# Products of ones on TensorE during the first loads, column sums of squares taken part by part, and late vectors loaded in the second step

## The chip, the cores and the metric

One core of a Trainium2 chip. The metric is the device time of one execution in microseconds. Below, PE is TensorE, DVE is VectorE, ACT is ScalarE, POOL is GpSimd and SP is SyncE, which issues most of the transfers.

## What is computed

One layer of a diffusion backbone over 512 latent tokens and 256 context tokens of width 1024, all in float32. The part that matters here is its beginning:

```
mod   = silu(c) @ w_ada + b_ada          # 6 x 1024: shift, scale, gate, twice
mod_c = silu(c_ctx) @ w_ada + b_ada
h     = rms_norm(x, norm1_g)   * (1 + scale1)   + shift1
hc    = rms_norm(ctx, norm1_g) * (1 + scale1_c) + shift1_c
q_c, kv_c, k_rope, ... = split(h @ w_in)         # 384, 256, 32, ... columns
q  = rms_norm(q_c,  q_norm_g)  @ w_uq
kv = rms_norm(kv_c, kv_norm_g) @ w_ukv           # the same for the context's kv
```

Attention over 8 heads, a gated linear attention branch, the merge of both, and a feed-forward with a 3x3 depthwise convolution (`conv_w`, `conv_b`) follow; they take most of the time and are not touched.

## The kernel before, in words

Every large product is made of three: each float32 operand is split into a high part (cast, on ScalarE) and a low part (subtraction, on VectorE or GpSimd), and `mm3` (line 144) multiplies high by high, high by low and low by high. `mm` (line 149) is one plain float32 product.

Lines 539 to 667 are the first stage, and its order is written out by hand: with an engine's name in `pinned`, the wrapper around every instruction (line 88) keeps it behind the engine's previous one. All five queues are pinned there; SP until line 667, POOL until 1026, VectorE and ScalarE until 1036, TensorE to the end. What is not pinned is placed by a scheduler. All operations come from that wrapper, so that the profile gives them line 88 (or 87), and tiles tell them apart.

The stage goes over eight slices j of 128 features. For each, `load_ada(j)` and `load_w(j)` issue two parts of `w_ada` (512 KB each) and the q and kv columns of `w_in` (320 KB) on SP, up to three steps ahead. `modulation(j)` (line 489) makes 8 float32 products of `silu(c)` with each part, in four column strips; VectorE copies the result; `factors(j)` (line 500) turns it with two small products into shift and scale per feature. `columns` (line 509) transposes the normalised tokens, `modulated` (line 517) applies shift and scale on ScalarE and splits on VectorE. `kv_latents` and `q_latents` (lines 528 and 533) accumulate the 256 kv columns in `accK` (two banks) and the 384 q columns in `accQ` (two banks, also called `two[1]`) and `accR`. `split_latents(j)` (line 389) splits the weights: casts on ScalarE, subtractions on POOL. Step 0 is done in two halves of 256 tokens (lines 572 to 592): modulation, transposes of two token rows, factors, 15 products of 256 columns; then the token rows 2 and 3 are normalised (lines 579 to 583), and the same again.

The small vectors come as rows into one tile `X0`: `c`, `c_ctx`, `norm1_g` and `b_ada` (ROWS[0:4]) issued on ScalarE, `q_norm_g`, `kv_norm_g`, `gla_norm_g`, `gla_b_decay`, `norm2_g` and `conv_b` (ROWS[4:], together 22 KB) and the two parts of `conv_w` (99 KB) on POOL, all at the start (lines 540 and 551). TensorE transposes the first 16 rows (line 555), the first 72 (line 566), and in step j = 3 the late ones (line 639). Neither kind of transpose nor the products wait for anything but their own operands and the instruction ahead of them.

After the loop (line 930), the squares of the kv latents are added over the two blocks and summed over the features with products by a column of ones (`totals`, line 674: one column per 128 tokens); `spread` (line 669) turns the reciprocal roots into rows. The same follows for q (three blocks, added on VectorE) and for the context's kv (two blocks in one bank), whose sums go into the last columns of `two[1]`, the bank that holds the second block of the q latents. `misc` (line 695) multiplies the rope and decay columns between them.

```
sk, sq = [EK() for _ in range(2)], []                                    # line 930
for k in range(2):
    A.activation(sk[k][:, 0:512], kb_[k], AF.Square)
tt(V, sk[0][:, 0:512], sk[0][:, 0:512], sk[1][:, 0:512], ALU.add)
...
totals(two[1][:, 512:], sq[0], 4)                                        # line 964
totals(two[1][:, 516:], sc, 2)
misc(0, 3, 8)
```

`smask` is the second half of the tile `WD`; the linear attention fills it with ones and zeros (line 1052) and reads it after the attention heads.

Of the kernel before, what the change touches and what calls it, by code (L numbers as in the profile page):

```python
# [13 lines left out]
ALU = mybir.AluOpType  # L14
# [56 lines left out]
def block_kernel(ctx: ExitStack, tc: tile.TileContext, p, out):  # L71
# [58 lines left out]
    def f(ap):  # L130
        return ap.bitcast(F32)
# [17 lines left out]
    def mm(o, a, b, first=True, last=True):  # L149
        PE.matmul(o, lhsT=a, rhs=b, start=first, stop=last)  # L150
# [184 lines left out]
    with tc.tile_pool(name="e1", bufs=1) as e1:  # L335
# [11 lines left out]
        G.memset(f(WD), 0.0)  # L347
# [141 lines left out]
        def modulation(j):  # L489
            for i in range(2):  # L490
                for rnd in range(2):
                    for g in range(4):
                        kt = 2 * g + rnd
                        mm(mp[32 * g:32 * g + 32, 128 * i:128 * i + 128], cstat[:, kt, :], ada[j][i][:, kt, :], rnd == 0,
                           rnd == 1)
            rows = EP()[:, 0:256]
            V.tensor_copy(rows, mp[:, 0:256])
            return rows
# [39 lines left out]

        pinned |= {"PE", "V", "A", "G", "SY"}
        for i_, (name, k) in enumerate(ROWS):  # L540
            load_rows((A if i_ < 4 else G), name, k)
# [9 lines left out]
        for (dst, a, b) in ((pw[:, 0, :], 0, 128), (pw[0:70, 1, :], 128, 198)):  # L551
            G.dma_start(out=dst, in_=p["conv_w"][0].rearrange("a b (c d) -> (a b c) d", d=128)[a:b])

        ps_ = single[1]
        PE.transpose(ps_[:, 0:16], pk[0:16, :], ident[0:16, 0:16])
        cc = pcol[:, 0:16]
# [9 lines left out]
        PE.transpose(single[2][:, 0:NROW1], pk[0:NROW1, :], ident[0:NROW1, 0:NROW1])  # L566
        V.tensor_copy(pcol[:, 16:NROW1], single[2][:, 16:NROW1])
# [6 lines left out]
        factors(0, rows)  # L574
        split_latents(0)
# [22 lines left out]
        def extra_loads(j):  # L598
            if j == 1:
                load_ada(4)  # L600
# [29 lines left out]
        for j in range(1, 8):  # L630
# [8 lines left out]
            if j == 3:  # L639
                ps_ = single[2 - tps[0] % 2]  # L640
                n2 = NROWS - NROW1
                PE.transpose(ps_[:, 0:n2], pk2[0:n2, :], ident[0:n2, 0:n2])
                PE.transpose(ps_[:, 128:256], pw[:, 0, :], ident)
                PE.transpose(ps_[:, 256:326], pw[0:70, 1, :], ident[0:70, 0:70])
                V.tensor_copy(pcol[:, NROW1:NROWS], ps_[:, 0:n2])
                V.tensor_copy(cwT, ps_[:, 128:326])
# [27 lines left out]
        def totals(ss, sq, n):  # L674

            for t in range(n):
                mm(ss[:, t:t + 1], sq[:, t * 128:(t + 1) * 128], ones[:, 0:1])
# [255 lines left out]
        tt(V, sk[0][:, 0:512], sk[0][:, 0:512], sk[1][:, 0:512], ALU.add)  # L933
        q_latents(7, 0, 512)
        mwh, mwl = split_misc(mraw_[0])
        totals(sums, sk[0], 4)
# [15 lines left out]
        for k in range(2):  # L952
            V.scalar_tensor_tensor(out=kn[k][:, 0:512], in0=kb_[k], scalar=col("kv_norm_g", k), in1=rb[:, 0:512],
                                   op0=ALU.mult, op1=ALU.mult)
            A.copy(kvLh[:, k, :], kn[k][:, 0:512])
# [3 lines left out]
        sc = EK()  # L959
        A.activation(sc[:, 0:512], single[1], AF.Square)  # L960
        tt(V, sc[:, 0:256], sc[:, 0:256], sc[:, 256:512], ALU.add)
        q_latent(1)
        q_latent(2)
        totals(two[1][:, 512:], sq[0], 4)
        totals(two[1][:, 516:], sc, 2)
        misc(0, 3, 8)
        scaled(vq[:, 0:4], two[1][:, 512:516], 384)
        scaled(vq[:, 4:6], two[1][:, 516:518], 256)
# [82 lines left out]
    with tc.tile_pool(name="egl", bufs=1) as eg:  # L1051
        G.memset(smask, 1.0)
        G.memset(grp(smask, 4)[:, :, 0:1], 0.0)
        one_c = ones[:, 0:1].broadcast_to([128, 256])
# [512 lines left out]
```

## Time and profile before

| | |
|---|---|
| median of 3 runs | 915.4 us (912.56 to 915.64) |
| the profiled execution's own time | 913.15 us |
| its span, first to last instruction | 911.4 us |
| TensorE busy in the span | 886.5 us (97%) |
| VectorE, ScalarE, GpSimd busy | 580.1, 396.3, 372.6 us |
| mean granted clock of TensorE | 0.995 of full speed |

The profile shows one execution. Times in its rows count from the first instruction. A matmul's end is modelled and contains its way through the array, so the time of a stretch of products is read from start to start. The weight loads that go with the products have rows of their own and are left out here.

### The profile page before, as it was taken

How to read it: one execution, taken by the hardware profiler on the slowest of the kernel's cores; microseconds unless marked ns; L12 is line 12 of the kernel's file. 1: busy time of each engine (PE TensorE's matmuls, PEld its weight loads, DVE VectorE, ACT ScalarE, POOL GpSimd, SP SyncE). 2: the span in 40 equal slices, each digit the busy share in tenths (PEclk: the TensorE clock that was granted, in tenths of full speed). 3: DMA queues.
4: the chain of work that ended last, by engine and by line, in shares of the span. 5: the costliest groups of instructions: out<-in, count | busy, mean ns of one | idle time of the engine just before them, and what ended most of it. 6: DMA issues, size and time to landing. Idle time of an engine off the chain costs nothing.

```text
span 911.4 us, 12634 instructions
## 1 busy us (share of the span) xinstructions
PE 886.5 (97%) x4864; PEld 750.7 (82%) x4864; DVE 580.1 (64%) x971; ACT 396.3 (43%) x655; POOL 372.6 (41%) x223
## 2 busy tenths in 40 slices
PE   5999999999999999999999999999999999999996
PEld 4878899888888888888887889888888888888885
DVE  4567778874967777765674684988787776300006
ACT  4355667764344554534545333443333333322105
POOL 3422255460525252423554423343535444466403
PEclk9999999999999999999999999999999999999998
DMA  9940000216313233324972512434343432244102
GB/s 313 328 131 1 1 4 12 91 47 185 97 42 110 76 104 82 97 78 136 316 252 82 151 47 91 122 111 139 93 138 93 139 115 94 70 161 143 43 1 92
DMA packets 131436, 100.89 MB, mean 111 GB/s; under 512 B 6826, under 2 KB 121874, under 8 KB 131376
## 3 DMA queue, kind: packets, MB, share of 16 engines
q1 hardware_dynamic: 130256, 97.56, 34.9%
q0 software_dynamic: 864, 2.22, 0.7%
q8 instruction: 38, 0.62, 0.3%
q10 hardware_dynamic: 256, 0.30, 0.1%
q14 instruction: 22, 0.18, 0.1%
HBM read 97.78 MB, written 2.10 MB: 110 GB/s over the span
## 4 chain that ended last, share of the span: by engine, by line
PE 90%; DVE 4%; ACT 2%; issue 1%; POOL 1%; DMA 1%; SPq 0%; DVEq 0%; ACTq 0%; POOLq 0%
PE pb L88 47%; PE p L88 23%; PE pb L87 14%; PE p L87 6%; DVE s L88 1%; DMA raw<-in_w_ada_dram 1%; DVE kT L88 1%; ACT s L88 1%; ACT P L88 0%; DVE P L88 0%; DVE mx L88 0%; ACT kT L88 0%; POOL P L88 0%; POOL s L88 0%; POOL wlo L88 0%
## 5 line engine op out<-in xcount | busy, mean ns | idle before, releaser
L88 POOL TENSOR_TENSOR wlo<-raw,whi 128x1024 fp32r<-128x1024 f32 (+1 forms) x106 | 241.6, 2286 | 355.3 <-ACT whi L88 341.2
L88 PE MATMUL pb<-s,whi 128*128 128x512 f32 (+1 forms) x906 | 272.4, 383 | 0.0
L88 PEld LDWEIGHTS pb<-s,whi 128*128 128x128 f32 x906 | 167.6, 188 | 32.1
L88 ACT CAST whi<-raw 128x1024 fp32r<-128x1024 f32 (+1 forms) x106 | 103.4, 977 | 179.6 <-issue 77.6
L88 PE MATMUL pb<-s,wlo 128*128 128x512 f32 (+1 forms) x453 | 172.9, 382 | 0.0
L88 DVE SCALAR_TENSOR_TENSOR ac<-pb,cwT,ac 128x441 f32<-128x441 f32 (+2 forms) x160 | 111.0, 694 | 19.2 <-ACT ac L88 15.4
L87 PE MATMUL pb<-s,whi 128*128 128x512 f32 x320 | 101.7, 396 | 0.0
L88 PEld LDWEIGHTS pb<-s,wlo 128*128 128x128 f32 x453 | 85.3, 188 | 16.6
L88 PE MATMUL p<-s,s 128*128 128x512 f32 (+1 forms) x392 | 83.4, 369 | 1.7 <-DVE s L88 1.5
L88 PEld LDWEIGHTS p<-s,s 128*128 128x128 f32 x392 | 66.4, 191 | 14.9 <-DVE s L88 2.2
L87 PEld LDWEIGHTS pb<-s,whi 128*128 128x128 f32 x320 | 58.9, 188 | 12.4 <-issue 0.7
L88 PE MATMUL p<-whi,s 128*128 128x512 f32 x208 | 69.0, 393 | 0.1
L88 DVE TENSOR_TENSOR p<-p,gt 128x512 f32<-128x512 f32 x4 | 2.8, 699 | 98.5 <-PE p L88 98.4
L87 PE MATMUL pb<-s,wlo 128*128 128x512 f32 x160 | 62.8, 392 | 0.0
L88 PE MATMUL pb<-whi,s 128*128 128x512 f32 x176 | 57.6, 390 | 0.0
L88 PEld LDWEIGHTS p<-whi,s 128*128 128x128 f32 x208 | 39.1, 188 | 8.4 <-ACT s L88 0.4
L88 PE MATMUL pb<-s,s 128*32 128x128 f32 (+2 forms) x322 | 43.6, 335 | 0.9 <-DVE rv L88 0.9
L88 DVE TENSOR_TENSOR pl<-pb,ph 128x512 fp32r<-128x512 f32 x48 | 33.0, 687 | 14.8 <-ACT ph L88 14.5
L88 PE MATMUL p<-kT,s 128*128 128x512 f32 (+1 forms) x192 | 41.1, 350 | 0.9 <-ACT P L88 0.9
L88 PE MATMUL p<-wlo,s 128*128 128x512 f32 x104 | 40.5, 390 | 0.0
L88 ACT ACTIVATE ac<-ac 128x512 f32<-128x512 f32 x22 | 13.9, 632 | 59.6 <-DVE ac L88 59.6
L88 PEld LDWEIGHTS pb<-s,s 128*128 128x128 f32 (+1 forms) x322 | 34.1, 166 | 6.4 <-DVE rv L88 1.1
(250 smaller groups left out, 1558.4 us busy)
## 6 DMA issues: line engine op xcount, KB each, us to landing
raw<-in_w_up_dram SPq DMA_DIRECT2D x44, 512.0 KB, 3.7
raw<-in_w_in_dram SPq DMA_DIRECT2D x28, 512.0 KB, 3.7
raw<-in_w_down_dram SPq DMA_DIRECT2D x22, 512.0 KB, 3.6
s<-in_w_ada_dram SPq DMA_DIRECT2D x20, 512.0 KB, 5.9
raw<-in_w_ada_dram SPq DMA_DIRECT2D x18, 512.0 KB, 5.1
xn<-in_w_ada_dram SPq DMA_DIRECT2D x10, 512.0 KB, 5.1
kT<-in_w_in_dram SPq DMA_DIRECT2D x8, 320.0 KB, 6.9
s<-in_x_dram SPq DMA_DIRECT2D x4, 512.0 KB, 5.3
```

What stands on the lines that cost most here:

```text
L87: return fn(*args, **kw)
L88: ins = fn(*args, **kw)
```

## The change

Four kinds of edits. Thirteen float32 products of ones with ones (`fill`, into `accK`, which is begun anew before it is used) are placed between the first instructions of TensorE; the ones are `smask`, now filled by VectorE at the start, while POOL clears only the other half of `WD`. The rows ROWS[4:] and `conv_w` are issued by POOL in step j = 1, behind the subtractions of step 2's weights, and their transposes stand in step j = 5. The sums of squares of kv and of the context take the two blocks as two accumulating products instead of an addition on VectorE and one product; the context's squares are taken earlier on ScalarE; the sums of q and context go into `sums`. And the two instructions that fill `smask` for the linear attention are pinned.

```diff
--- before.py
+++ after.py
@@ -344,7 +344,8 @@
         pk, pk2, pw = X0[:, 0:128], X0[:, 128:256], grp(X0[:, 256:512], 2)
         kcos, ksin = tl(e1, [128, 512], F32, "pl", 2), tl(e1, [128, 512], F32, "pl", 2)
         V.memset(cstat, 0.0)
-        G.memset(f(WD), 0.0)
+        V.memset(smask, 1.0)
+        G.memset(f(wst), 0.0)
 
         def load_rows(eng, name, k):
             src = p[name]
@@ -488,6 +489,8 @@
 
         def modulation(j):
             for i in range(2):
+                if j == 0 and i == 1:
+                    fill(accK, 1, 128)
                 for rnd in range(2):
                     for g in range(4):
                         kt = 2 * g + rnd
@@ -536,9 +539,14 @@
                 ws = slice(k * 128, (k + 1) * 128)
                 mm3(qb_[k][:, a:b], wj[j][0][:, ws], wj[j][1][:, ws], h_, l_, j == 0 and a == 0, j == 7)
 
+        def fill(ps, n, width=256):
+
+            for _ in range(n):
+                mm(ps[:, 0:width], smask[:, 0:128], smask[:, 0:width])
+
         pinned |= {"PE", "V", "A", "G", "SY"}
-        for i_, (name, k) in enumerate(ROWS):
-            load_rows((A if i_ < 4 else G), name, k)
+        for name, k in ROWS[0:4]:
+            load_rows(A, name, k)
         SY.dma_start(out=cst[:, 0:130], in_=p["consts"][:, 0:130])
         load_x(0)
         load_x(1)
@@ -548,11 +556,12 @@
         load_x(3)
         load_ada(1)
         load_w(1)
-        for (dst, a, b) in ((pw[:, 0, :], 0, 128), (pw[0:70, 1, :], 128, 198)):
-            G.dma_start(out=dst, in_=p["conv_w"][0].rearrange("a b (c d) -> (a b c) d", d=128)[a:b])
-
+
+        fill(accK, 3)
+        fill(accK, 1, 128)
         ps_ = single[1]
         PE.transpose(ps_[:, 0:16], pk[0:16, :], ident[0:16, 0:16])
+        fill(accK, 2)
         cc = pcol[:, 0:16]
         V.tensor_copy(cc, ps_[:, 0:16])
         se, sc_ = sm(16, "se", 1), sm(16, "sc_", 1)
@@ -564,6 +573,7 @@
         tt(V, cstat[:, :, 1], cc[:, 8:16], sc_[:, 8:16], ALU.mult)
         ss = squared(0)
         PE.transpose(single[2][:, 0:NROW1], pk[0:NROW1, :], ident[0:NROW1, 0:NROW1])
+        fill(accK, 1)
         V.tensor_copy(pcol[:, 16:NROW1], single[2][:, 16:NROW1])
         for dst, j in ((b1sc, 8), (b2sc, 32)):
             V.tensor_scalar(out=dst, in0=pcol[:, ROW0["b_ada"] + j:ROW0["b_ada"] + j + 8], scalar1=1.0, scalar2=None,
@@ -572,6 +582,7 @@
         rows = modulation(0)
         tp = columns(0, 0, 0, 2)
         factors(0, rows)
+        fill(accK, 5, 128)
         split_latents(0)
         modulated(0, 0, 0, 2, tp)
         kv_latents(0, 0, 256)
@@ -597,6 +608,10 @@
 
         def extra_loads(j):
             if j == 1:
+                for name, k in ROWS[4:]:
+                    load_rows(G, name, k)
+                for (dst, a, b) in ((pw[:, 0, :], 0, 128), (pw[0:70, 1, :], 128, 198)):
+                    G.dma_start(out=dst, in_=p["conv_w"][0].rearrange("a b (c d) -> (a b c) d", d=128)[a:b])
                 load_ada(4)
                 load_w(4)
                 load_x(4)
@@ -636,7 +651,7 @@
                 V.tensor_scalar(out=xs[j], in0=xs[j], scalar1=rc[:, j - 4:j - 3], scalar2=None, op0=ALU.mult)
             elif j == 7:
                 context(4, 8)
-            if j == 3:
+            if j == 5:
                 ps_ = single[2 - tps[0] % 2]
                 n2 = NROWS - NROW1
                 PE.transpose(ps_[:, 0:n2], pk2[0:n2, :], ident[0:n2, 0:n2])
@@ -674,7 +689,8 @@
         def totals(ss, sq, n):
 
             for t in range(n):
-                mm(ss[:, t:t + 1], sq[:, t * 128:(t + 1) * 128], ones[:, 0:1])
+                for i, s_ in enumerate(sq):
+                    mm(ss[:, t:t + 1], s_[:, t * 128:(t + 1) * 128], ones[:, 0:1], i == 0, i == len(sq) - 1)
 
         def scaled(v, ss, width):
             V.tensor_scalar(out=v, in0=ss, scalar1=-0.5 / width, scalar2=-0.5 * EPS, op0=ALU.mult, op1=ALU.add)
@@ -930,10 +946,9 @@
         sk, sq = [EK() for _ in range(2)], []
         for k in range(2):
             A.activation(sk[k][:, 0:512], kb_[k], AF.Square)
-        tt(V, sk[0][:, 0:512], sk[0][:, 0:512], sk[1][:, 0:512], ALU.add)
         q_latents(7, 0, 512)
         mwh, mwl = split_misc(mraw_[0])
-        totals(sums, sk[0], 4)
+        totals(sums, sk, 4)
         scaled(vk, sums[:, 0:4], 256)
         ctx_latents(0, 4)
         sq.append(EK())
@@ -952,20 +967,20 @@
         for k in range(2):
             V.scalar_tensor_tensor(out=kn[k][:, 0:512], in0=kb_[k], scalar=col("kv_norm_g", k), in1=rb[:, 0:512],
                                    op0=ALU.mult, op1=ALU.mult)
+            if k == 0:
+                sc = EK()
+                A.activation(sc[:, 0:512], single[1], AF.Square)
             A.copy(kvLh[:, k, :], kn[k][:, 0:512])
         for k in range(2):
             sub(V, kvLl[:, k, :], kn[k][:, 0:512], f(kvLh[:, k, :]))
         misc(0, 0, 3)
-        sc = EK()
-        A.activation(sc[:, 0:512], single[1], AF.Square)
-        tt(V, sc[:, 0:256], sc[:, 0:256], sc[:, 256:512], ALU.add)
         q_latent(1)
         q_latent(2)
-        totals(two[1][:, 512:], sq[0], 4)
-        totals(two[1][:, 516:], sc, 2)
+        totals(sums, sq[0:1], 4)
+        totals(sums[:, 4:], [sc, sc[:, 256:]], 2)
         misc(0, 3, 8)
-        scaled(vq[:, 0:4], two[1][:, 512:516], 384)
-        scaled(vq[:, 4:6], two[1][:, 516:518], 256)
+        scaled(vq[:, 0:4], sums[:, 0:4], 384)
+        scaled(vq[:, 4:6], sums[:, 4:6], 256)
         rq = rstd_exp(None, 6, None, vq)
         split_wq(2)
         spread(sums, rq[:, 4:6], 2)
@@ -1049,8 +1064,10 @@
     G.dma_start(out=gt1, in_=p["b_ada"][0:1, 2048:3072].broadcast_to([128, 1024]))
 
     with tc.tile_pool(name="egl", bufs=1) as eg:
+        pinned.add("G")
         G.memset(smask, 1.0)
         G.memset(grp(smask, 4)[:, :, 0:1], 0.0)
+        pinned.discard("G")
         one_c = ones[:, 0:1].broadcast_to([128, 256])
 
         def E2(tag, n, bufs):
```

## Rows read from the trace of the kernel before

**Rows 1.** The page's chain of work that ended last, as shares of the span by engine.

```profile
PE 90%; DVE 4%; ACT 2%; issue 1%; POOL 1%; DMA 1%; SPq 0%; DVEq 0%; ACTq 0%; POOLq 0%
```

**Rows 2.** Timeline of TensorE, first 40 us. Columns: start (us), time to the end of the last of the group (us), engine, line, operation, output<-inputs, stationary rows*columns, shape of the moving part, count, and in brackets the idle time before and what ended it. A group merges equal instructions in a row; an f32 product is two instructions, a transpose one.

```profile
4.96 0.25 PE L88 MATMUL pb<-cst,X 16*128 16x16 f32 x1 [4.96 <-DMA X<-in_c_ctx_dram]
7.87 0.35 PE L88 MATMUL pb<-cst,X 72*128 72x72 f32 x1 [2.65 <-DMA X<-in_b_ada_dram]
9.12 1.08 PE L88 MATMUL pb<-s,s 128*32 128x128 f32 x16 [0.90 <-DVE rv L88]
10.70 1.08 PE L88 MATMUL pb<-raw,s 128*32 128x128 f32 x16 [0.50 <-DMA raw<-in_w_ada_dram]
...
12.33 1.02 PE L88 MATMUL pb<-cst,P 128*128 128x2 f32 x4
14.83 1.90 PE L88 MATMUL p<-s,s 128*128 128x256 f32 x6 [1.49 <-DVE s L88]
...
18.58 1.08 PE L88 MATMUL pb<-s,s 128*32 128x128 f32 x16
...
20.45 1.20 PE L88 MATMUL pb<-cst,s 128*128 128x128 f32 x6
...
22.12 1.32 PE L88 MATMUL p<-s,s 128*128 128x256 f32 x6
...
24.36 0.60 PE L88 MATMUL pb<-cst,s 128*128 128x128 f32 x4
24.89 0.65 PE L88 MATMUL pb<-s,s 128*32 128x128 f32 x16
...
25.90 1.66 PE L88 MATMUL p<-s,s 128*128 128x512 f32 x6
27.40 0.50 PE L88 MATMUL pb<-cst,P 128*128 128x2 f32 x4
...
37.43 1.64 PE L88 MATMUL p<-s,s 128*128 128x512 f32 x6
```

**Rows 3.** Timeline of VectorE (DVE), first 45 us, same columns.

```profile
10.09 1.42 DVE L88 TENSOR_SCALAR s<-s,rr 128x1024 f32<-128x1024 f32 x2
11.85 0.42 DVE L88 COPY P<-pb 128x256 f32<-128x256 f32 x1 [0.35 <-PE pb L88]
13.39 0.22 DVE L88 TENSOR_SCALAR shc<-pb,pcol 128x2 f32<-128x2 f32 x1 [1.11 <-PE pb L88]
...
14.81 0.43 DVE L88 TENSOR_TENSOR s<-P,s 128x256 fp32r<-128x256 f32 x1
...
18.62 0.75 DVE L88 TENSOR_SCALAR s<-s,rr 128x1024 f32<-128x1024 f32 x1
```

**Rows 4.** Timeline of TensorE, 60 to 85 us, same columns.

```profile
65.18 1.05 PE L88 MATMUL pb<-ones,kT 128*128 128x1 f32 x8 [0.90 <-DVE kT L88]
66.10 3.12 PE L88 MATMUL pb<-s,s 128*128 128x256 f32 x24
...
76.49 1.50 PE L88 MATMUL p<-ones,kT 128*128 128x1 f32 x12 [1.26 <-DVE s L88]
77.85 5.28 PE L88 MATMUL pb<-s,s 128*128 128x512 f32 x15
82.96 1.50 PE L88 MATMUL pb<-cst,rr 128*128 128x128 f32 x12
```

**Rows 5.** Windows view of two stretches: from:to (us), length, busy time of PE, PEld, DVE, ACT and POOL with the number of instructions, granted clock of TensorE as a share of full speed, DMA share, GB/s.

```profile
40.00:50.00 10.00, 10.00 (x104) 7.98 (x104) 6.72 (x14) 4.40 (x10) 5.58 (x7) 1.00 1.05 306
...
80.00:81.00 1.00, 1.00 (x4) 0.81 (x3) 0.79 (x2) 0.00 (x0) 0.00 (x0) 0.50 0.00 0
```

**Rows 6.** Timeline of TensorE around the one f32 product of 256 columns with ones in the feed-forward stage (`mod_bcast`).

```profile
607.13 0.39 PE L88 MATMUL pb<-s,wlo 128*128 128x512 f32 x1
607.36 0.59 PE L88 MATMUL pb<-mp,ones 128*128 128x256 f32 x2
...
608.25 0.40 PE L88 MATMUL pb<-s,wlo 128*128 128x512 f32 x1
```

**Rows 7.** Timeline of SyncE's issues (SPq): start, time the issue held the queue, transfer.

```profile
8.91 2.19 SPq L88 DMA_DIRECT2D raw<-in_w_ada_dram  x1
```

**Rows 8.** The view of one tensor, `in_w_ada_dram`, first 60 us: from issue to landing, of 16 transfers.

```profile
DMA to landing us min/median/max: 5.2/6.9/8.1
```

**Rows 9.** Timeline of GpSimd (POOL), first 45 us, columns as in rows 2; a DMA row is the time that the issue takes on GpSimd.

```profile
24.93 1.45 POOL L88 TENSOR_TENSOR wlo<-kT,whi 128x384 fp32r<-128x384 f32 x1
29.59 0.74 POOL L88 TENSOR_TENSOR s<-kT,s 128x256 fp32r<-128x256 f32 x1 [3.20 <-ACT s L88]
...
44.52 0.73 POOL L88 DMA_DIRECT2D qtab<-in_consts_dram  x1
```

**Rows 10.** Timeline of VectorE, 64 to 77 us.

```profile
64.44 0.68 DVE L88 TENSOR_TENSOR kT<-kT,kT 128x512 f32<-128x512 f32 x1
...
75.22 0.42 DVE L88 TENSOR_TENSOR kT<-kT 128x256 f32<-128x256 f32 x1
75.68 0.75 DVE L88 SCALAR_TENSOR_TENSOR s<-p,pcol,s 128x512 fp32r<-128x512 f32 x1
```

**Rows 11.** Timeline of ScalarE (ACT), 71 to 75 us.

```profile
71.64 0.59 ACT L88 COPY P<-pb 128x512 f32<-128x512 f32 x1
...
74.48 0.60 ACT L88 ACTIVATE kT<-pb 128x512 f32<-128x512 f32 x1
```

## The prediction

> **What bounds the kernel now.** I read the chain of waits first. TensorE holds 90% of what ended last [rows 1], so the end moves only where TensorE idles, runs at a lower clock, or gets more or less work. I then looked for those places in its timeline. There are two.
>
> The first is the start [rows 2]. Up to 14.83 us TensorE waits for small loads, weights and VectorE: 4.96, 2.65, 0.90, 0.50 and 1.49 us of idle time ahead of the rows shown. From there the work is dense, but slow. The 15 products of 14.83 to 18.58 us take 3.75 us; the same 15 from 22.12 to 24.36 us take 2.24 us; both include a short wait for the low half, a subtraction of 0.43 us [rows 3]. The 32 modulation products take 1.87 us from 18.58 us and 1.01 us from 24.89 us. 15 x 256 columns in 3.75 us less 0.4 are 1.15 columns per ns, about the lower of the two clock levels, 1.2 GHz; afterwards the rate is about double. (The granted clock shows no value below 1.00 in this stretch, so I go by the durations.) The rise thus comes near 22 us, after some 7 us of dense products.
>
> The second is 64 to 83 us, where the latents' squares are summed [rows 4]. TensorE waits 0.90 us for an addition of squares, later 1.26 us for VectorE, and soon after that the granted clock is 0.50 [rows 5]: 15 products of 512 columns take from 77.85 to 82.96 us, 5.11 us. At the upper level one takes 0.23 us (607.13 to 607.36 us, [rows 6]), 15 take 3.4; the lower level costs 1.7 us.
>
> **The fills, and what they cost.** 13 products of ones are added: six 256 wide, seven 128 wide. The nearest row is the f32 product with ones, 256 columns wide, in the feed-forward: from 607.36 to 608.25 us there lie this product and two of 0.225 us, so it takes 0.44 us at the upper level [rows 6]; I put 0.88 us at the lower, and half of each for 128 columns. All 13 are 8.4 us at the lower level and 4.2 us at the upper, against 10.5 us of idle time. Group by group at the lower level, the ones being ready near 1.7 us (VectorE is idle there, so their memset costs nothing): three and a half end at 4.8 us, before the load of 4.96 us; two from 5.2 us end at 7.0, before 7.87; one from 8.2 us ends at 9.1, at the 9.12 us product; the small one between the halves of the modulation ends at 10.5, before 10.70. The last five lie behind the factors: at the lower level they run from 13.35 to 15.5 us, 0.7 us past the start of the 14.83 us products; at the upper from 12.5 to 13.6 us, and cost nothing. Only products behind them on TensorE wait for a fill.
>
> **What they bring.** I take the clock to be up by 11 to 14 us, since from 8.2 us on fills, transposes and modulation leave almost no gap; the bound on the other side is a rise near 22 us as now. With it up, the first modulation ends near 11.3 us, the copy of its rows follows VectorE's scaling, at 11.5 us instead of 11.85 [rows 3], the factors take 0.5 us as at 27.40 us (1.02 at 12.33, [rows 2]), and their readers on VectorE start at 12.55 instead of 13.39 us. So the products of 14.83 us start at 14.0. What is late next is not TensorE: its 15 and 32 products would be through at 17.3 us, but rows three and four of x are normalised behind the factors' readers on ScalarE and VectorE, to 19.37 us now [rows 3], to 18.5 us then. The transposes of 20.45 us start at 18.55, 1.9 us earlier; they and what follows are 0.3 us shorter, so 24.36 us becomes 22.15. I put **2.2 us**. Bounds: 0.7 us lost (the five fills late, no rise) and 3.5 us won (both stretches at double rate, no chain in the way).
>
> Do the loads allow it? The modulation weights issued at 8.91 us [rows 7] land at most 8.1 us later [rows 8], at 17.0 us, just where they would be used then; later ones are issued up to three steps ahead. A wait of 0.3 us here would lie inside the 18.5 us that VectorE sets.
>
> **The row loads.** Eight issues leave GpSimd's first microseconds (121 KB) and return behind its low-half subtractions of step 2, which end at 26.4 us now, 24.2 then [rows 9]. At 0.73 us each, the longest such row, they end at 30.0 us. The next subtraction, due at 27.4 us then, waits behind them and ends at 30.8 us; its reader, the product of 37.43 us [rows 2], then at 35.2, has 4 us left. The transposes that read the rows move two steps on, to about 46 us, 8 us after the last landing. Early on, 121 KB at the 306 GB/s of [rows 5] are at most 0.4 us less ahead of the first weights; between 0 and 0.4 I take 0, since the chain above goes by x, which is issued ahead of most of them. GpSimd's smaller memset and its pinned later one lie in idle time.
>
> **The sums of squares.** First place: the addition of 0.68 us goes [rows 10], and the column sums double from 8 to 16 instructions of 0.115 us (0.92 us for 8, [rows 4]): from 64.28 they end at 66.1, as now. Nothing is gained; VectorE comes 0.68 us earlier, and TensorE does not wait for it there. Second place: the sums go into a bank that VectorE reads until 76.43 us [rows 10], hence the 1.26 us. The new bank has its last reader at 71.64 to 72.23 us [rows 11]. The context squares move ahead on ScalarE, from 74.48 us to about 73.3; the high halves behind them slip 0.6 us, and VectorE, rid of an addition of 0.42 us, reaches its q latents as now. So the sums start at 75.2 and their 16 instructions (12 now) end at 77.0 instead of 77.85: **0.9 us**. The scale factors are ready near 78.5 us, and the products in between hold TensorE until 80.5, so no new wait. Bounds: 1.3 us (the whole gap) and nothing.
>
> **The clock there.** After 64.28 us there are 1.8 us without dense products, and the clock stayed up; after 75.2 there are 2.6, and it fell. With 1.8 us in the second place too, I take it to stay: **1.7 us**, with 0 as the other end.
>
> **Sum.** 2.2 + 0.9 + 1.7 = 4.8 us off the profiled execution's 913.15: 908.3. The median of the runs shown lies 2.25 us above that execution, and the runs spread over 3.1 us; a clock that rises or falls at another moment could do that, and the fills should take part of it away. I put 910.0, between 908.3 and the median less 4.8, 910.6.
>
> The Trainium skill, "TensorE: Matmul & The Clock Gate", Part 1, says that the lower rate is the default and activity releases it, with which the start agrees. A remark there puts the ramp at under 1% of a typical span and warns against fitting it to one count; by it the 2.2 us could be anything from nothing to 3.5 us, which the range holds.
>
> **Rivals.** *The clock falls again in the second place.* Sixteen one-column instructions in a row remain there, and one stretch that stayed up is thin evidence. Then the 1.7 us stay: 911.7. *The fills don't bring the rise forward.* Until 8 us they leave gaps of 0.9 us, and the nearly dense 14.83 to 18.23 us brought no rise by itself. Then the start gains nothing: 912.2; with both, 913.9. *Slower: GpSimd's issues take far longer in step 2*, with the DMA queues full, than at the start; SyncE's issue at 8.91 us took 2.19 us [rows 7]. From 1.3 us per issue on, the subtraction of step 3 ends after 35.2 us and TensorE waits; at 2.2 us each it ends at 42.5, 7 us late, and the time is 917; at 2.6 us, 920.5. Against it: the issue of 44.52 us took 0.73 us [rows 9], with the DMA share at 1.05 and VectorE busy for 6.7 of 10 us [rows 5]. The Trainium skill, "DMA: Bandwidth & Descriptors", section SWDGE vs HWDGE vs iDMA, says that GpSimd writes its descriptors into memory out of which VectorE can lock it; by that page this rival would be likelier. That row does not show it.
>
> **How the numbers follow.** Forecast 0.50; second fall 0.20; no earlier rise 0.15; both 0.07; GpSimd's issues 0.05; something else 0.03. Range 906.5 to 914.7: below, 908.3 with a start 1.3 us better and 0.4 us of loads; above, both rivals and 0.8 us. About 0.5% (4.6 us) is what a measurement of this kernel can tell from no change; faster by that is under 910.8. Of the forecast 0.36 lie there, of the second fall 0.06, of the late rise 0.03: 0.45 in all. Slower by it is over 920: 0.05 with what is unforeseen. Same: 0.50.
>
> **What would show it.** Right: the first 15 products in little over 2 us; the transposes of 20.45 us near 18.5, with TensorE idle for about a microsecond ahead of them; no gap before the second column sums; a granted clock of 1.00 from 75 to 85 us; the subtractions of step 3 near 30 us. Wrong: the first 15 products still at 3.7 us, a clock of 0.50 after the sums, or TensorE waiting for GpSimd near 35 us.

## The result, and the profile after

The changed kernel takes 907.67 us as the median of 4 runs (906.89 to 909.06), the kernel before 915.52 us (4 runs, 912.56 to 916.02). The ratio is 0.9923, 95% interval 0.9897 to 0.9948. The profiled execution took 906.93 us (span 905.1 us, mean granted clock 0.998), 6.22 us less than the profiled execution before (913.15 us).

TensorE's timeline at the start, against [rows 2]:

```profile
1.76 3.36 PE L88 MATMUL p<-s 128*128 128x256 f32 x8 [1.76 <-DVE s L88]
5.05 0.28 PE L88 MATMUL pb<-cst,X 16*128 16x16 f32 x1
5.26 2.08 PE L88 MATMUL p<-s 128*128 128x256 f32 x4
7.13 0.33 PE L88 MATMUL pb<-cst,X 72*128 72x72 f32 x1
7.25 0.92 PE L88 MATMUL p<-s 128*128 128x256 f32 x2
8.47 0.65 PE L88 MATMUL pb<-s,s 128*32 128x128 f32 x16 [0.30 <-DMA s<-in_w_ada_dram]
9.05 0.49 PE L88 MATMUL p<-s 128*128 128x128 f32 x2
9.87 0.64 PE L88 MATMUL pb<-raw,s 128*32 128x128 f32 x16 [0.34 <-DMA raw<-in_w_ada_dram]
...
11.11 0.61 PE L88 MATMUL pb<-cst,P 128*128 128x2 f32 x4
11.58 1.36 PE L88 MATMUL p<-s 128*128 128x128 f32 x10
13.20 1.31 PE L88 MATMUL p<-s,s 128*128 128x256 f32 x6 [0.26 <-DVE s L88]
...
15.51 0.65 PE L88 MATMUL pb<-s,s 128*32 128x128 f32 x16
...
17.80 0.76 PE L88 MATMUL pb<-cst,s 128*128 128x128 f32 x5 [0.72 <-DVE s L88]
...
19.11 1.32 PE L88 MATMUL p<-s,s 128*128 128x256 f32 x6 [0.21 <-DVE s L88]
...
21.35 0.60 PE L88 MATMUL pb<-cst,s 128*128 128x128 f32 x4
```

The rows `p<-s` are the fills. An f32 product is two instructions. The two products of 256 columns at 5.26 us still take 1.87 us up to the next row, 0.94 us each; the one at 7.25 us is through after 0.92 us with its way through the array, and the modulation behind it runs at the upper rate (0.65 us, not 1.08): the rate rises there. The first 15 products take 2.31 us (13.20 to 15.51), not 3.75. At 17.80 us TensorE waits for VectorE: that wait was not there before.

VectorE, against [rows 3]. The normalisation of the last of x's four token rows (16.99 us) ends at 17.74 us, and that is what the wait ahead of 17.80 us is for:

```profile
9.31 1.42 DVE L88 TENSOR_SCALAR s<-s,rr 128x1024 f32<-128x1024 f32 x2
...
16.99 0.75 DVE L88 TENSOR_SCALAR s<-s,rr 128x1024 f32<-128x1024 f32 x1
```

TensorE where the squares are summed, against [rows 4]. No idle time stands before either row of one-column products, and the 15 products of 512 columns take 3.54 us (73.27 to 76.81), not 5.11:

```profile
61.07 1.84 PE L88 MATMUL pb<-ones,kT 128*128 128x1 f32 x16
62.77 3.12 PE L88 MATMUL pb<-s,s 128*128 128x256 f32 x24
...
71.57 1.84 PE L88 MATMUL pb<-ones,kT 128*128 128x1 f32 x16
73.27 3.71 PE L88 MATMUL pb<-s,s 128*128 128x512 f32 x15
76.81 1.50 PE L88 MATMUL pb<-cst,rr 128*128 128x128 f32 x12
```

The windows view of the same stretch, against [rows 5] (columns as there): the granted clock is 1.00.

```profile
74.00:78.00 4.00, 4.00 (x24) 3.45 (x24) 2.77 (x7) 1.73 (x5) 0.00 (x0) 1.00 0.00 0
```

GpSimd's moved issues, against [rows 9]: 0.52 to 0.72 us each, and the subtraction of step 3 starts at 28.03 us:

```profile
23.60 0.72 POOL L88 DMA_DIRECT2D X<-in_q_norm_g_dram  x1
...
26.90 1.11 POOL L88 DMA_DIRECT2D X<-in_conv_w_dram  x2
28.03 0.74 POOL L88 TENSOR_TENSOR s<-kT,s 128x256 fp32r<-128x256 f32 x1
```

The difference of the two profiles can be laid out by marks that both have. Start of step 1: 24.36 against 21.35 us, 3.01 us. From there to the last q product (63.90 against 60.84 us): 0.05 us. From there to 82.96 against 76.81 us: 3.09 us, of which 1.57 us are the clock. To the end: 0.1 us. So in this pair of executions nearly all of it arises at the two places that the change touches. How much of it is the change's, the experiments say.

### The profile page after: what moved, and what is told of

The parts are those of the page before. It is cut to its first block, busy times and chain, and to the rows that moved or that the text cites. A ratio compares the mean times of both kernels' runs of the same rounds, so it can differ in the third digit from the quotient of the medians.

```text
span 905.1 us, 12711 instructions
## 1 busy us (share of the span) xinstructions
PE 889.3 (98%) x4902; PEld 753.4 (83%) x4902; DVE 577.2 (64%) x970; ACT 395.8 (44%) x655; POOL 370.5 (41%) x223
## 4 chain that ended last, share of the span: by engine, by line
PE 92%; DVE 3%; ACT 2%; issue 1%; POOL 1%; DMA 1%; SPq 0%; ACTq 0%; DVEq 0%; POOLq 0%
PE pb L88 49%; PE p L88 23%; PE pb L87 14%; PE p L87 6%; DMA raw<-in_w_ada_dram 1%; DVE s L88 1%; ACT P L88 0%; DVE kT L88 0%; DVE mx L88 0%; ACT s L88 0%; DVE P L88 0%; POOL P L88 0%; POOL s L88 0%; POOL wlo L88 0%; ACT kT L88 0%
## 5 line engine op out<-in xcount | busy, mean ns | idle before, releaser
L88 PE MATMUL pb<-s,s 128*32 128x128 f32 (+2 forms) x322 | 41.1, 315 | 0.3 <-DMA s<-in_w_ada_dram 0.3
L88 PEld LDWEIGHTS pb<-whi,s 128*128 128x128 f32 x176 | 33.1, 188 | 6.9
```

The lines of the kernel that those rows point to most:

```text
L88: ins = fn(*args, **kw)
```

## The experiments

Each line is against the kernel before on the same chip; there were three chips, and the second column has the median of the kernel before on each. The ratio has its own estimate and is not the quotient of the two medians. The last column is the mean granted clock of the timed executions; 0.998 is what is left when the clock falls only at the end of the program, as in the profile of the changed kernel. It is a rough sign: it doesn't say where the clock fell, or whether TensorE's time mattered there. The fastest execution of "whole, again", 906.75 us, has 0.995.

| run | kernel before, us | median us (range) | ratio, 95% interval | clock |
|---|---|---|---|---|
| fills alone | 911.84 | 910.16 (908.37 to 911.58) | 0.9986, 0.9975 to 0.9997 | 0.994 to 0.998 |
| row loads alone | 911.84 | 911.32 (909.33 to 912.2) | 0.9996, 0.9986 to 1.0007 | 0.995 to 0.997 |
| sums alone | 911.84 | 908.79 (908.09 to 909.99) | 0.9974, 0.9965 to 0.9983 | 0.997 to 0.998 |
| whole without fills | 911.84 | 908.28 (907.83 to 908.73) | 0.9969, 0.9959 to 0.998 | 0.998 |
| whole | 913.73 | 908.47 (907.01 to 909.01) | 0.9931, 0.9916 to 0.9945 | 0.995 to 0.998 |
| other bank alone | 913.73 | 912.26 (908.88 to 914.11) | 0.9976, 0.996 to 0.9992 | 0.995 to 0.998 |
| gaps filled alone | 913.73 | 909.87 (909.53 to 911.25) | 0.9951, 0.9937 to 0.9965 | 0.997 to 0.998 |
| whole without the last five fills | 913.73 | 907.32 (907.16 to 908.35) | 0.9925, 0.991 to 0.994 | 0.994 to 0.996 |
| whole and four fills in the new wait | 914.67 | 907.18 (906.88 to 907.9) | 0.9934, 0.9914 to 0.9954 | 0.995 to 0.998 |
| whole without fills, again | 914.67 | 910.29 (908.39 to 912.37) | 0.9964, 0.995 to 0.9978 | 0.996 or 0.998 |
| whole, again | 914.67 | 907.02 (906.75 to 908.86) | 0.9936, 0.9917 to 0.9956 | 0.995 to 0.998 |
| whole with twelve fills for five | 914.67 | 906.94 (906.88 to 906.97) | 0.9929, 0.9912 to 0.9947 | 0.997 to 0.998 |

**The parts.** Fills alone: the kernel before with every `fill` of the diff and its memsets.

> The kernel before with the 13 products of ones alone (and the ones' memset). Theory A, the start is won by the clock and by earlier loads as two separate terms: the first 15 products take about 2.2 us instead of 3.75, the start of step 1 (24.36 us before, 21.35 after the whole change) comes near 22.1, a gain of 2.2 us; the sums of squares and their low clock stay as before: 911 in a profile, 913 as median. Rival B, the fills do all of the start: 21.4 us, a gain of 3.0. Rival C, fills are held up by the loads they stand between and lose what the clock gives: under 1 us.

1.7 us as medians; that contains what the ones' memsets do near 230 us (the last paragraph of this section). Its profile starts step 1 at 21.20 us, as rival B had it, though the row loads stand where they stood before. What that says of the loads comes below. The granted clock is up throughout 60 to 80 us in this execution, with the gaps of 0.93 and 1.25 us still there:

```profile
73.31 1.50 PE L88 MATMUL p<-ones,kT 128*128 128x1 f32 x12 [1.25 <-DVE s L88]
74.67 3.67 PE L88 MATMUL pb<-s,s 128*128 128x512 f32 x15
```

The mean clocks of 0.994 to 0.996 in ten of the twelve timed executions say that it mostly falls somewhere, not where.

Row loads alone: POOL's eight issues and their transposes moved as in the diff.

> The kernel before with the late vectors alone moved to step 1 (their transposes to step 5). Theory A: x's second tile and the first modulation weights land 0.8 to 1.0 us earlier, TensorE's first 15 products start 0.8 us earlier at 14.0 us, at the lower clock; step 1 starts at 23.5 us: gain 0.8 us, 914.7 as median. Rival B, as predicted blind: the 121 KB are 0 to 0.4 us: 915.2 to 915.5. Rival D: without fills an earlier start finds the same moment of the rise, so that nothing is left at 24.36 us.

0.5 us as medians, with an interval from 1.3 us won to 0.6 us lost: the time can't tell the prediction's 0 to 0.4 us from theory A's 0.8 us. The landing of the loads speaks against theory A. In the four profiles of this chip the second half of the first modulation, the product that waits for the weights, starts at 9.63 us (fills alone) and 9.69 us (sums alone) with the rows loaded early, at 9.59 us (row loads alone) and 9.33 us (whole without fills) with them late. It starts at 10.70 us in [rows 2] and at 9.87 us in the changed profile. So the 0.83 us between those two are mostly how fast the loads came in two executions, not the change.

Sums alone: `totals` with both blocks, the other bank, the earlier squares.

> The kernel before with the sums of squares alone changed (two accumulating products, their bank, the earlier squares of the context). Theory A: the gaps ahead of both sums go, 0.3 us and 1.25 us, and the clock stays up behind the second, 1.6 us more: 3.1 us, 912.4 as median, granted clock 1.00 from 75 to 85 us. Rival E: the clock falls there all the same, since its fall depends on the moment: 1.5 us, 914.0.

3.05 us as medians, theory A's number (1.6 to 3.2 us by the interval). The clock stays up: in this profile the 15 products take 3.54 us, and on this chip the mean clock is 0.997 to 0.998 in all 21 executions of the two kernels with the new sums (sums alone, whole without fills) and 0.995 to 0.997 in all 45 of the two with the old ones (before, row loads alone). These two pairs have neither fills nor the ones' memsets. This is the largest single part that was taken by itself.

**The wait and the bank.** The kernel before, with the sums written elsewhere and nothing else:

```diff
-        totals(two[1][:, 512:], sq[0], 4)
-        totals(two[1][:, 516:], sc, 2)
+        totals(sums, sq[0], 4)
+        totals(sums[:, 4:], sc, 2)
```

> The kernel before, but the sums of q and of the context go into the other bank; additions, instructions and the time of the context's squares stay. Theory A: TensorE's wait of 1.25 us before the second column sums was for the reader of the old bank; it now waits for the context's squares and their addition, which end some 0.5 us earlier: gap near 0.8 us, gain 0.5 us in the profile; the clock can still fall there. Rival G, the wait was for the squares all along: no gain.

The timeline of TensorE in its profile:

```profile
68.73 5.19 PE L88 MATMUL pb<-s,s 128*128 128x256 f32 x33
73.76 1.39 PE L88 MATMUL pb<-ones,kT 128*128 128x1 f32 x12
75.01 3.71 PE L88 MATMUL pb<-s,s 128*128 128x512 f32 x15
```

The wait of 1.26 us in [rows 4] is gone entirely, with the additions still on VectorE: it was for the old bank's reader. Theory A had the cause, and the gain too small; rival G is out. The 12 instructions take 1.25 us here, the 16 of the whole change 1.70 us. At this place, then, summing part by part costs 0.45 us of TensorE; what it does save is the addition's place in VectorE's queue. At the first place it removes the wait of 0.90 us and adds 8 instructions: from the last q product to the products behind the sums 2.20 us before (63.90 to 66.10), 1.93 us after (60.84 to 62.77).

What each part is worth can be read from one stretch, that from the last q product to the row of twelve transposes behind the 15 products. It takes 19.06 us before; 17.50 us in the profile of the fills alone, where both gaps stand and the clock stays up (60.69 to 78.19); 16.02 us with the other bank alone, where it stays up as well (62.54 to 78.56); and 15.97 us with the whole change. So in these profiles the low clock is worth 1.56 us, the other bank 1.48 us, and the sums part by part with the earlier squares 0.05 us.

**The clock at the sums.** The kernel before with products of ones in the two gaps, and none at the start (not printed here: `fill`, the ones and their memsets, which are as in the whole change):

```diff
+        fill(single[2], 2)
         totals(sums, sk[0], 4)
...
+        fill(accK, 2)
+        fill(accK, 1, 128)
         totals(two[1][:, 512:], sq[0], 4)
```

> The kernel before with products of ones in the two gaps ahead of the column sums alone (two of 256 columns in the first; two and a half in the second) and none at the start. Theory A, the clock falls when the gap and the one-column products together leave TensorE without dense work for about 2.6 us: with the gaps filled it stays up in every run (mean clock 0.998), and the time falls by the 1.6 us of the low clock, in those runs that had it: 910.2 as median, although no instruction of the sums starts earlier. Rival E, the one-column products alone bring the fall, or its moment is chance: clock 0.996 or less in some runs, time unchanged near 911.8.

TensorE's timeline and the windows view of its profile:

```profile
73.62 1.25 PE L88 MATMUL p<-s 128*128 128x256 f32 x6
75.04 1.50 PE L88 MATMUL p<-ones,kT 128*128 128x1 f32 x12 [0.17 <-DVE s L88]
76.40 3.71 PE L88 MATMUL pb<-s,s 128*128 128x512 f32 x15
```

```profile
70.00:80.00 10.00, 9.82 (x58) 8.51 (x57) 7.60 (x16) 5.12 (x11) 0.00 (x0) 1.00 0.01 2
```

The sums start no earlier, and TensorE computes nothing useful in the gaps, yet the kernel is 3.9 us faster as medians, with a mean clock of 0.997 to 0.998 in every execution. Idle time next to one-column products is what lets the clock fall there, and either place can be the one: in the profile of the row loads alone it fell at the first place. Timeline and windows view of that execution:

```profile
62.98 1.05 PE L88 MATMUL pb<-ones,kT 128*128 128x1 f32 x8 [0.93 <-DVE kT L88]
63.90 4.32 PE L88 MATMUL pb<-s,s 128*128 128x256 f32 x24
```

```profile
66.00:69.00 3.00, 3.00 (x17) 3.00 (x16) 2.38 (x6) 2.40 (x7) 0.00 (x0) 0.54 0.00 0
```

How long the sparse stretch is does not settle it. Here the clock fell behind 0.93 us of idle time and 8 instructions; in the profile of the fills alone it stayed up behind 1.25 us and 12, the very stretch behind which it fell in [rows 4]. So theory A's 2.6 us are no limit, and of the three profiles that still have both gaps unfilled (before, row loads alone, fills alone) two show a fall. In all nine profiles with the new sums, 16 instructions without idle time twice over, there is none.

3.9 us is more than the clock at one place is worth; this kernel also has the memsets, and the last paragraph of this section has the rest.

**The start.** The changed kernel without its fills, on two chips:

> The changed kernel without its 13 products of ones. Theory A (terms add up): loses 2.2 us against the changed kernel's 907.7: 909.9; the rise of the clock back near 21 us, the first 15 products at 3.4 us or more. Rival B: loses all 3.0 us of the start: 910.7.

> The changed kernel without its products of ones, now on the same chip as the whole change. Theory I: the fills win 1.6 us in the runs where the clock then stays up and next to nothing where it falls again; as medians 0.5 to 1.0 us: this kernel lies that much above the whole change, with mean clock 0.998 throughout. The blind step (2.2 us from the fills) wants 2.2 us.

And the whole change on the two other chips:

> The whole change, beside the kernel before on the same chip. Theory A, the terms of the parts add up (1.7 us of fills, 0.5 of row loads, 3.05 of sums, as medians against the same kernel before): 5.2 us less, about 906.6 where before is 911.8. Rival F, the fills and the sums both save the same moments of low clock: 3.6 us for rows and sums, and at most 1 us more for fills, 907.3 to 908.3. The 7.85 us seen first would then hold some 2.5 us that are not the change's.

> The whole change again, as the measure for the other three: 4 to 5 us below the kernel before; runs in two groups, near 907 (clock up) and near 908.5 to 909 (mean clock 0.995 to 0.997).

As medians the whole change is 5.3 us below the kernel before on one chip, near theory A's 5.2, and 7.6 us on the other; it was 7.85 us in the first comparison. On the last chip the fills with their memsets are worth 3.3 us (910.29 less 907.02), more than the 0.5 to 1.0 us of theory I or the 2.2 us of the prediction, and the mean clock without them is 0.996 in five of twelve executions; the last paragraph of this section has the reason. On the first chip no direct comparison was made. The traces price the fills alone. In the profiles of the whole change without fills step 1 starts at 22.96 and 22.90 us, in all six profiles without fills at the start, other than that of [rows 2], at 22.17 to 23.08 us. In these six the rate rises between some 17 and 19.5 us, in [rows 2] only near 21 us. So 1.4 of the 3.0 us by which the changed profile started step 1 earlier belong to that one execution of the kernel before, and the fills won some 1.6 us.

With fills step 1 starts at 21.35 us (first profile), but at 22.67 and 22.35 us in the two later ones. The reason is in the profile of 908.99 us. Timeline of TensorE and windows view:

```profile
17.80 0.77 PE L88 MATMUL pb<-cst,s 128*128 128x128 f32 x5 [0.76 <-DVE s L88]
...
19.11 1.84 PE L88 MATMUL p<-s,s 128*128 128x256 f32 x6 [0.21 <-DVE s L88]
...
22.67 0.80 PE L88 MATMUL pb<-cst,s 128*128 128x128 f32 x4
```

```profile
20.00:23.00 3.00, 3.00 (x16) 3.00 (x16) 1.30 (x2) 1.53 (x3) 1.76 (x3) 0.50 1.15 340
```

Behind the wait for the normalised rows the clock has fallen to its lower level, and the second 15 products take 3.56 us, not 2.24: 1.3 us are given back. Step 1, begun at the lower level, takes 0.2 us longer, and step 2 takes 6.04 us, not 5.57. VectorE and GpSimd there:

```profile
28.24 2.39 DVE L88 TENSOR_TENSOR s<-P,s 128x512 fp32r<-128x512 f32 x1
...
28.37 0.74 POOL L88 TENSOR_TENSOR s<-kT,s 128x256 fp32r<-128x256 f32 x1
```

VectorE's subtraction takes 2.39 us; in the first profile it took 1.16 us (from 26.71 us). As TensorE is late, VectorE's subtraction now stands beside one that GpSimd begins as soon as the moved row loads are issued. That the one stretches the other is argued from the times. The other late profile has the same (2.35 us from 28.21 us). The last q product, behind which these profiles agree, starts at 62.84 and 62.74 us in these two, at 60.84 us in the first, and at 62.45 and 62.40 us without fills. Where the clock falls again, the fills win nothing, as theory I had it.

Of the 16 executions of the whole change eight lie at 906.75 to 907.1 us and eight at 908.36 to 909.06 us. Whether that wait is to blame, two kernels tell. One fills it; one puts the work elsewhere, with seven fills more behind the factors:

```diff
         rows = modulation(1)
+        fill(single[2], 4, 128)
         tp = columns(0, 0, 2, 2)
```

> The whole change, with four more products of ones (128 columns) in the wait that opened ahead of the second transposes (16.7 to 17.7 us), written into a bank that is free there. Theory I, the early rise is given back where TensorE waits for the normalised rows of x and the clock falls again in some runs: with the wait filled it stays up in every run, mean clock 0.998, step 1 starts at 21.4 us in every profile, 907.0 as median and a narrower spread; 0 to 1.5 us better than the whole change. Rival J, the second fall was chance and has nothing to do with this wait: the same spread and median as the whole change.

```diff
         factors(0, rows)
-        fill(accK, 5, 128)
+        fill(accK, 12, 128)
```

> The whole change with twelve products of ones of 128 columns behind the first factors, not five. They end near 14.2 us at the upper clock, so that the first 15 products start 1.0 us later. Theory K, VectorE's normalisation of x's rows three and four sets the next start: the second transposes still come at 17.8 us, the wait ahead of them goes, and the time is the same as the whole change or, by theory I, up to 1 us better as the clock stays up. Rival L, every added product on the path is paid: 1.0 us slower.

TensorE's timeline with twelve fills:

```profile
11.60 2.92 PE L88 MATMUL p<-s 128*128 128x128 f32 x24
14.28 0.96 PE L88 MATMUL p<-s,s 128*128 128x256 f32 x6
...
17.82 0.77 PE L88 MATMUL pb<-cst,s 128*128 128x128 f32 x5 [0.25 <-DVE s L88]
...
21.36 0.60 PE L88 MATMUL pb<-cst,s 128*128 128x128 f32 x4
```

The first products start 1.1 us later than with five fills, and everything from 17.82 us on is where it was: VectorE sets the next start, and 1.1 us of added products cost nothing. The six executions lie within 0.09 us, 906.88 to 906.97 us. With four fills in the wait three of six executions are at 907.35 to 907.9 us with clocks of 0.995 to 0.997, and why is open. The three medians of this chip (906.94, 907.02 and 907.18 us) can't be told apart; the spread can: none of these twelve executions lies above 907.9 us, eight of the 16 of the whole change do (two of six on this chip). That speaks for theory I, the wait as the cause of the second fall, and against rival L.

The opposite was tried too, the whole change without the five fills behind the factors:

> The whole change without the five products of ones behind the first factors. Theory A, the clock is up by then and stays up without them: the same as the whole change within 0.3 us. Rival H, they hold the clock up over the wait for ScalarE and VectorE: without them it falls or rises late, 1.5 to 2 us lost.

```profile
13.20 1.89 PE L88 MATMUL p<-s,s 128*128 128x256 f32 x6 [1.49 <-DVE s L88]
...
16.94 0.64 PE L88 MATMUL pb<-s,s 128*32 128x128 f32 x16
...
21.61 0.60 PE L88 MATMUL pb<-cst,s 128*128 128x128 f32 x4
```

```profile
14.00:17.00 3.00, 3.00 (x18) 2.78 (x21) 1.85 (x8) 1.85 (x6) 0.00 (x0) 0.50 1.12 364
```

Rival H is right about the clock: it had risen by 7 us, fell behind the wait of 1.49 us, and the 15 products take 3.74 us again. Theory A is nearer about the time: step 1 starts only 0.26 us later than in the first profile of the whole change, because there TensorE waits for VectorE until 17.80 us anyway. The slower products fill that wait, and the clock does not fall again in this profile. As medians this kernel is even 1.15 us below the whole change on its chip (907.32 against 908.47 us; ranges 907.16 to 908.35 and 907.01 to 909.01). So the five fills by themselves win nothing that shows.

**Why the medians differ by more than the profiles.** The kernel without fills took 908.28 us on one chip and 910.29 on another. Its two profiles differ in the decay gates' stage near 230 us. VectorE there, first in the execution of 908.73 us, then in that of 912.09 us:

```profile
230.21 0.35 DVE L88 TENSOR_SCALAR mp<-s,csilu 128x256 f32<-128x256 f32 x1
230.47 2.63 DVE L88 SCALAR_TENSOR_TENSOR mp<-s,csilu,mp 128x256 f32<-128x256 f32 x1
```

```profile
230.12 2.58 DVE L88 TENSOR_SCALAR mp<-s,csilu 128x256 f32<-128x256 f32 x1
232.62 2.61 DVE L88 SCALAR_TENSOR_TENSOR mp<-s,csilu,mp 128x256 f32<-128x256 f32 x1
```

GpSimd begins a subtraction of some 2.5 us at 230.25 us in the first and at 230.14 us in the second, 0.04 and 0.02 us behind the same VectorE instruction. In the second that instruction takes 2.58 us instead of 0.35, and the products that need its sum come too late. TensorE in the second, and its clock after that:

```profile
240.32 0.74 PE L88 MATMUL pb<-ones,mp 128*128 128x1 f32 x4 [1.79 <-DVE mp L88]
```

```profile
241.00:244.00 3.00, 3.00 (x15) 3.00 (x15) 2.19 (x6) 0.00 (x0) 0.00 (x0) 0.50 0.67 175
```

A wait of 1.8 us and a low clock behind it, 3.4 us between the two executions (912.09 less 908.73), go with a difference of 0.02 us. The Trainium skill, "SBUF — State Buffer", section Who interferes with whom, says that VectorE and GpSimd share a port pair as an exclusive lock, held for a whole instruction by whichever came first. The length agrees with that, 2.58 us beside GpSimd's 2.5; the order does not, for by the start times of the trace VectorE came first. The profile of the other bank alone has the same wait, with a distance of 0.03 us. The sums alone and the row loads alone, like the first of these two, have 0.04 us and no wait. In the eight profiles with the ones' memsets (the one for the linear attention, pinned, runs at 194.83 us in the changed profile; before it ran at 6.04 us), GpSimd starts 0.09 to 0.11 us behind, and none has the wait. Other than these memsets the eight kernels share only that they have products of ones, some at the start, one at the sums. So a second effect of the change, which no part of the prediction names, may be this distance; no run moves the memsets by themselves, and how one at 194.83 us would shift a start at 228.64 us is open, so that is argued, not shown. That the kernel before loses time there in many of its executions is argued from its times, up to 916.1 us, and its mean clocks of 0.993 to 0.994: its one profile does not have the wait.

## Why the prediction was right, and where it was not

The measured 907.67 us lies in the range of 906.5 to 914.7 us, below the forecast of 910.0; faster was the smaller of the two likely outcomes, 0.45 against 0.50.

*The fills' price and place* were nearly right. At the lower level 256 columns took 0.94 us, not 0.88, so that in the changed profile the first two groups end at 5.05 and 7.13 us, no sooner than the rows had landed (no wait for a load stands before either transpose); the next product waits for its weights until 8.47 us, and nothing is lost. At the upper level twelve fills of 128 columns took 2.68 us, 0.22 us each, as taken. The clock rises even earlier than taken, between some 5 and 8 us.

*The start, 2.2 us*: right in mechanism, 3.01 us in the pair of profiles, but that is in part luck. The chain came as forecast: transposes behind VectorE's normalisation with about a microsecond of idle TensorE ahead of them (0.72 us). Yet the step measured from one execution with a late start; against the other profiles without fills the term is some 1.6 us. What the step missed besides is the second half of the story: it named the new wait and did not ask what the clock does in it. There it falls in two of three profiles, and by the times in about half of the executions; 1.9 to 2.0 us are gone by the last q product, all that the fills had won.

*The five fills behind the factors* were costed as free at the upper clock and 0.7 us at the lower. They are free even if they end a microsecond late, as twelve of them show, because VectorE sets the next start.

*The sums, 0.9 us*: mis-sized, 1.52 us in the profiles. The other bank, which the step named as the reason, makes 1.48 us by itself. The first place gave 0.27 us, not nothing: 16 instructions take 1.70 us, 0.106 us each, not 0.115. The second, from 70.05 and 66.54 us to the 15 products, gave 1.07 us, not 0.9, and the products between the two 0.18 us. *The clock there, 1.7 us*: 1.57 us, and in all twelve executions of the sums alone it is not below 0.997. The rival in which it falls again did not come. The reason given, a stretch of 1.8 us that kept the clock and one of 2.6 us that lost it, was luck: in two other profiles the same stretches did the opposite. What the runs show is that the clock did not fall where the idle time was gone.

*GpSimd's issues*: 0.52 to 0.72 us in step 2, as taken; the slower rival needed 1.3 us each. The Trainium skill, "DMA: Bandwidth & Descriptors", section SWDGE vs HWDGE vs iDMA, by which that rival would be likelier, is not borne out by these rows.

*From the profile to the median*: of the 2.25 us the forecast let about a quarter go (910.6 to 910.0), for a clock that rises or falls at another moment. That was right in kind: executions of one kernel differ by it. Another part, the meeting of VectorE and GpSimd near 230 us, was not seen, because the one profile of before does not have it. So the sum of 4.8 us is near what the parts show (some 1.6 us for the fills where the clock holds, 1.5 for the sums, 1.6 for the clock), while the 7.85 us of the medians holds more than this sum foresaw; on another chip the whole change gave 5.3 us.

## What to carry to other kernels

Products of ones are worth placing wherever TensorE waits beside sparse work, but count what they win up to the next engine's wait, and look whether that wait lets the clock fall again: seven more fills ahead of it cost nothing and made the time steady, five alone won nothing that shows. A small result written into a bank that another engine still reads is a wait that no arithmetic explains; writing it elsewhere removed 1.26 us by itself. And compare parts on one chip, with the clock of every execution beside its time: the same kernel before took 911.8 to 915.5 us here, and the one execution whose profile was read had the latest start of seven.

## What the runs showed of the hardware

The granted clock fell to 0.50 behind quite different stretches: 8 one-column instructions after 0.93 us of idle time, 12 after 1.26 us, a wait of 1.49 us behind factors, one of 0.76 us between modulation and transposes. In other profiles with the same stretches (1.25 us and 12 instructions, a wait of 0.72 us) it did not fall there; and in nine profiles it did not fall behind 16 such instructions without idle time, 1.70 us. A VectorE instruction of 0.35 us took 2.58 us when GpSimd began a long subtraction 0.02 or 0.03 us behind it, and 0.35 us when that was 0.04 to 0.11 us. A longer one, a subtraction of 512 columns, took 2.35 and 2.39 us when GpSimd's began 0.09 and 0.13 us behind it, and 1.16 us in the first profile of the changed kernel.
